# The split activations of the gate and up products: two long runs instead of sixteen interleaved pairs

## The chip, the cores and the metric

The kernel runs on one core of a Trainium2 chip. The metric is the time of one execution in device microseconds (us); lower is better. Five engines work side by side: TensorE does the matrix products (the profile calls its products PE and its weight loads PEld), VectorE is DVE, ScalarE is ACT, GpSimd is POOL, and SyncE (SP) issues most of the transfers. Operands lie in on-chip memory with 128 partitions; an address here always means a byte offset inside a partition.

## The reference, cut to what matters

One decoder block is computed for 256 tokens with 16 meta tokens ahead of them: a projection, two token mixers, a merge, and a feed-forward part. The change touches the feed-forward part alone:

```python
merged = g_a * (y_a @ w_a) + g_b * (y_b @ w_b)
h = h + merged @ w_o
gate, up = jnp.split(_rms(h, n2) @ w_gu, 2, axis=-1)      # w_gu: 2048 x 11264
return h + (jax.nn.silu(gate) * up) @ w_dn                # w_dn: 5632 x 2048
```

All inputs are float32, and the first 16 positions are dropped from the output.

## The kernel before, in words

Every large product is made from split operands. A float32 value is written as a high part, which is the value rounded to the type `float32r`, and a low part, which is the rest. A product then needs three terms: high by high, high by low, and low by high.

**Weights.** `wload` fetches a block of 1024 weights per partition into `raw` (a 512 KB transfer that SyncE issues), ACT writes the high part into `wh` (L335) and DVE the low part into `wl` (L336). There are four buffers of each of the three tiles, so the loads run a few blocks ahead of TensorE.

**Gate and up.** `cm_jobs` holds the weights still in the array and streams the activations past them. For gate and up a block is two channel tiles of 128 rows by 512 columns. The 2048 channels are 16 channel tiles, counted by `kt`. TensorE takes the four column groups `m` of a block in turn, and inside a group the two channel tiles `k`, one even and one odd. For each of these, `mm2` issues two products. The first (L441) loads a 128x128 piece of `wh` and streams 512 elements past it, 256 of the high and 256 of the low part of the activations, so that high and low results land side by side in one accumulation bank. The second (L443) loads the matching piece of `wl` and streams the 256 high elements again. For the last channel tile, 15, the order is turned round: the `wl` product first (L440), the `wh` product after it (L441). Gate and up are 11 pairs of jobs (`gt0`, `up0`, `gt1`, ...) of 8 blocks each. That is 22 x 4 x 16 = 1408 pairs of a 512-element and a 256-element product. `halves` adds up the two halves of a bank afterwards.

**The activations.** `hts` holds both parts of all 16 channel tiles. It is written once, behind the product with `w_o` (jobs `wo0` to `wo3`): each tile is transposed, scaled and split into `hts` by `post` in the `w_o` loop (ACT writes the high part, DVE the low part; both are recorded at the lines of the helper `split`, L510 and L511). Its shape is `[P, KT, 2, L]` with L = 272, although only the last 256 of the 272 elements of each row are used:

```python
hts = hp.tile([P, KT, 2, L], F32R, tag="hts", name="hts")
split(hts[:, k, 0, NMETA:], hts[:, k, 1, NMETA:], tmp)
a = act[:, kt, :, n0:n0 + n]          # in cm_jobs, with n0 = NMETA = 16, n = 256
```

So channel tiles are 2 x 272 x 4 = 2176 bytes apart, and the low part lies 1088 bytes behind the high part. In the built program the tile begins at byte 75,648 of each partition, which is 128 modulo 256. The high part of tile `kt` therefore begins at 192 modulo 256 where `kt` is even and at 64 where it is odd. The low part begins 64 further on, at 0 and at 128.

**The weights' places.** The default layout `PLACE = (0, 16, 24)` puts the pieces of `wh` at 192 and those of `wl` at 224 modulo 256, for even and odd tiles alike.

**Down.** After gate and up, the buffer of `hts` is used again as `sst` for sums of the feed-forward activations. In `w_o` and down products (`tm_jobs`, `product`) the roles are exchanged: the weights stream and the activations are held still.

The order of TensorE's instructions is the order in which the program issues them. Streams of small work are put between the products by a clock that the program keeps while it is built; nothing in it looks at addresses.

Of the kernel before, what the change touches and what calls it, by code (L numbers as in the profile page):

```python
# [10 lines left out]
F32R = mybir.dt.float32r  # L11
# [7 lines left out]
P = 128  # L19
D = 2048  # L20
NMETA = 16

T = 256
L = NMETA + T
# [3 lines left out]
DFF = 5632  # L28
# [6 lines left out]
KT = D // P  # L35
# [23 lines left out]
PLACE = (0, 16, 24)  # L59
APART = (1, 32, 32)  # L60
PLACE_T = (8, 16)

LANES = 108
BETWEEN = 2
# [52 lines left out]
def hybrid_block(ctx, tc, A, out, dbg=None):  # L117
# [18 lines left out]
    def aux_ps(name):  # L136
        return psa.tile([P, 512], F32, tag="aux", name=name)
# [88 lines left out]
    def vc(name, i=0):  # L226
        c = COLS[name] + i
        return vcol[:, c:c + 1]
# [132 lines left out]
    def kblock(ap):  # L361
        return ap.rearrange("(k p) c -> p k c", p=P)

    def mm3(ps, wh, wl, ah, al, first, last):
        nc.tensor.matmul(ps, wh, ah, start=first, stop=False)  # L365
        nc.tensor.matmul(ps, wh, al, start=False, stop=False)  # L366
        nc.tensor.matmul(ps, wl, ah, start=False, stop=last)  # L367
# [29 lines left out]
    def slot(ns):  # L397


        clock[0] += ns  # L400
        if clock[0] < clock[1]:
            return
        due = sorted((st for st in streams if st[0] <= clock[0]), key=lambda st: st[0])
        group = []
        for st in due:
            if st[2] and st[2][0] == "fox":
                mate = [c for c in streams if c[2] and c[2][0] == "chain" and st[2][1] + c[2][1] <= 8 - PSM]
                if mate and mate[0][0] > clock[0] and clock[0] < st[0] + HOLD and mate[0][0] < st[0] + HOLD:
                    continue
                group = [c for c in mate if c[0] <= clock[0]] + [st]  # L410
            else:
                group = [st]
                if st[2]:
                    group += [c for c in due if c[2] and c[2][0] == "fox" and st[2][1] + c[2][1] <= 8 - PSM][:1]
            break
        if group:
            clock[2] = 0.0
            for st in group:
                stage(st)
            clock[1] = clock[0] + max(GAP, MIX * clock[2])  # L420

    def finish_job():
        if pending:
            pending.pop()()

    def run(jobs):
        for load, mul in jobs:
            w = load()
            finish_job()
            pending.append(lambda w=w, mul=mul: mul(w))  # L430
# [6 lines left out]
    def mm2(ps, wh, wl, act, first, last):  # L437

        if last:
            nc.tensor.matmul(ps[:, :T], wl, act[:, 0, :], start=False, stop=False)  # L440
        nc.tensor.matmul(ps.rearrange("p (a t) -> p a t", a=2), wh, act, start=first, stop=last)  # L441
        if not last:
            nc.tensor.matmul(ps[:, :T], wl, act[:, 0, :], start=False, stop=False)  # L443

    def halves(dst, ps):

        nc.scalar.activation(dst, ps[:, :T], AF.Copy)
        nc.vector.tensor_tensor(dst, dst, ps[:, T:], op=ALU.add)

    def cm_jobs(wap, nk, act, n0, n, post, alloc=main_ps, name="cm", two=True, lay=PLACE):  # L450


        box = []
        cols = wap.shape[1]
        nm, kb = cols // P, 1024 // cols

        def mk(q):
            def load():
                return wload([(P, 0, [kb, cols], [((ALL,), kblock(wap[q * kb * P:(q + 1) * kb * P, :]))])], 1024,
                             lay=lay)  # L460

            def mul(w):
                (wh, wl), = w
                if q == 0:
                    box.extend(alloc(f"{name}_{m}") for m in range(nm))
                for m in range(nm):
                    ms = slice(m * P, (m + 1) * P)
                    for k in range(kb):
                        kt = q * kb + k
                        a = act[:, kt, :, n0:n0 + n]  # L470
                        if n == T and two:
                            mm2(box[m], wh[:, k % 2, k // 2, ms], wl[:, k % 2, k // 2, ms], a, kt == 0, kt == nk - 1)
                        else:
                            mm3(box[m][:, :n], wh[:, k % 2, k // 2, ms], wl[:, k % 2, k // 2, ms], a[:, 0], a[:, 1],
                                kt == 0, kt == nk - 1)
                        slot(3 * n / 2.4)
                if q == nk // kb - 1:
                    post(box)
            return load, mul
        return [mk(q) for q in range(nk // kb)]  # L480
# [28 lines left out]
    def split(hi, lo_, src):  # L509
        nc.scalar.activation(hi, src, AF.Copy)  # L510
        nc.vector.tensor_tensor(lo_, src, hi.bitcast(F32), op=ALU.subtract)  # L511
# [169 lines left out]
    def rwkv_jobs(g):  # L681
# [14 lines left out]
        for nm, off, full in (("k", 1024, True), ("v", 2048, True), ("r", 0, False)):  # L696
            n0, n = (0, L) if full else (14, T + 2)
            jobs += cm_jobs(w_in[:, off + c0:off + c0 + 256], KT, xhl, n0, n, post(nm, off, full), name=f"{nm}{g}", lay=APART)
# [512 lines left out]
    gt = None  # L1211
# [36 lines left out]
    gt = gt_pool.__enter__()  # L1248
# [52 lines left out]
    hp = hp_pool.__enter__()  # L1301
    hh = hp.tile([P, 2, D], F32, tag="hh", name="hh")

    hts = hp.tile([P, KT, 2, L], F32R, tag="hts", name="hts")
    ss2 = hp.tile([P, 2, 4], F32, tag="ss2", name="ss2")
    rs2 = hp.tile([P, 2], F32, tag="rs2", name="rs2")
    rsb2 = hp.tile([P, T], F32, tag="rsb2", name="rsb2")

    def tm_jobs(wap, nk, ah, al, post, name, lay=PLACE_T):

# [26 lines left out]
    for j in range(4):  # L1337
        js = slice(j * 512, (j + 1) * 512)
        nc.sync.dma_start(hh[:, :, js], x[:, js].rearrange("(t p) c -> p t c", p=P))

        def post(t, ps, j=j, js=js):
            nc.vector.tensor_tensor(hh[:, t, js], ps, hh[:, t, js], op=ALU.add)
            jk = hp.tile([P, 512], F32, tag="jk", name=f"jk{j}{t}", bufs=2)
            nc.scalar.activation(jk, hh[:, t, js], AF.Square, accum_out=ss2[:, t, j:j + 1])
            if t == 0:
                return
            for k in range(4 * j, 4 * j + 4):
                pt = aux_ps(f"hT{k}")[:, :T]
                for t in range(2):
                    nc.tensor.transpose(pt[:, t * P:(t + 1) * P], hh[:, t, k * P:(k + 1) * P], ident)  # L1350
                tmp = hp.tile([P, T], F32, tag="htmp", name=f"htmp{k}", bufs=3)
                nc.vector.tensor_scalar(tmp, pt, vc("n2", k), None, op0=ALU.mult)
                split(hts[:, k, 0, NMETA:], hts[:, k, 1, NMETA:], tmp)
        run(tm_jobs(A["w_o"][0][:, js], KT, mgh, mgl, post, f"wo{j}"))
    finish_job()
    nc.vector.tensor_reduce(rs2, ss2, axis=AX.X, op=ALU.add)
# [27 lines left out]
    wgu = A["w_gate_up"][0]  # L1384
    for j in range(DFF // 512):
        gs = [hp.tile([P, T], F32, tag="ga", name=f"ga{j}{m}", bufs=8) for m in range(4)]

        def post_gate(pss, gs=gs):
            for g, ps in zip(gs, pss):
                halves(g, ps)  # L1390
                nc.vector.tensor_tensor(g, g, rsb2, op=ALU.mult)
                nc.scalar.activation(g, g, AF.Silu)

        def post_up(pss, gs=gs, j=j):
            for m, (g, ps) in enumerate(zip(gs, pss)):
                ub = hp.tile([P, T], F32, tag="ub", name=f"ub{j}{m}", bufs=2)
                halves(ub, ps)
                nc.vector.tensor_tensor(ub, ub, rsb2, op=ALU.mult)
                nc.vector.tensor_tensor(ub, ub, g, op=ALU.mult)
                split(ach[:, 4 * j + m, :], acl[:, 4 * j + m, :], ub)  # L1400
        run(cm_jobs(wgu[:, j * 512:(j + 1) * 512], KT, hts, NMETA, T, post_gate, name=f"gt{j}"))
        run(cm_jobs(wgu[:, DFF + j * 512:DFF + (j + 1) * 512], KT, hts, NMETA, T, post_up, alloc=aux_ps, name=f"up{j}"))

# [5 lines left out]
    fast = FAST  # L1411
    slow = [i for i in range(NF // 2) if i not in fast]
    acp_h, acp_l = (t.rearrange("p (i k) (t c) -> p i k t c", k=2, t=2) for t in (ach, acl))
    sst = hp.tile([P, KT, 2, L], F32R, tag="hts", name="sst").rearrange("p k a t -> p (k a t)")
    sst = sst[:, :len(fast) * 6 * P].rearrange("p (i s a c) -> p i s a c", i=len(fast), s=3, a=2)

    def sums_of_pairs():
# [47 lines left out]
    def split_tiles():  # L1465
        return [wp.tile([P, WCOLS], F32R, tag=t, name=t, bufs=WB).rearrange("p (r c) -> p r c", c=L)[:, :, s:s + T]
                for t, s in zip(("wh", "wl"), PLACE_T)]

    def slow_jobs(i, cg, cs, end):
        def mk(x_):  # L1470
            def load():
                j = 2 * cg + x_
                return wload([(P, 0, [2, 512], [((ALL,), kblock(wdn[i * 256:(i + 1) * 256, j * 512:(j + 1) * 512]))])],
                             1024, lay=(None, *PLACE_T))

# [160 lines left out]
```

## Time and profile before

| | |
|---|---|
| median of 3 timed runs | 1520.99 us (1520.26 to 1521.58) |
| span of the profiled execution | 1517.7 us, from its first to its last instruction |
| TensorE products, share of the span | 99% |
| DVE, ACT | 73%, 53% |
| TensorE clock granted | full in all 40 slices |

The profiled execution gives its span alone as its own time; the timed runs lie 2.6 to 3.9 us above it, which is what stands around the first and the last instruction. The duration of a TensorE product in the trace contains a tail during which the next product already streams: products start about 0.23 and 0.12 us apart and last about 0.39 and 0.28 us. What counts is the distance from start to start.

### The profile page before, as it was taken

How to read it: one execution, taken by the hardware profiler on the slowest of the kernel's cores; microseconds unless marked ns; L12 is line 12 of the kernel's file. 1: busy time of each engine (PE TensorE's matmuls, PEld its weight loads, DVE VectorE, ACT ScalarE, POOL GpSimd, SP SyncE). 2: the span in 40 equal slices, each digit the busy share in tenths (PEclk: the TensorE clock that was granted, in tenths of full speed). 3: DMA queues.
4: the chain of work that ended last, by engine and by line, in shares of the span. 5: the costliest groups of instructions: out<-in, count | busy, mean ns of one | idle time of the engine just before them, and what ended most of it. 6: DMA issues, size and time to landing. Idle time of an engine off the chain costs nothing.

```text
span 1517.7 us, 26174 instructions
## 1 busy us (share of the span) xinstructions
PE 1509.9 (99%) x10071; PEld 1339.5 (88%) x10071; DVE 1112.0 (73%) x2009; ACT 808.3 (53%) x1230; POOL 99.3 (7%) x182
## 2 busy tenths in 40 slices
PE   9999999999999999999999999999999999999998
PEld 9999999999989888998888888888888888887887
DVE  7888699689789857875665666566566658879776
ACT  7664565475465545644554555454455545554543
POOL 2112202202202000000000000000000000000000
PEclk9999999999999999999999999999999999999999
DMA  8557456646645757777566666666666666566664
GB/s 271 166 166 212 119 156 185 170 122 173 188 127 149 223 152 214 234 231 240 181 179 192 189 187 193 191 186 192 190 187 191 193 186 182 178 211 201 213 206 138
DMA packets 210365, 283.32 MB, mean 187 GB/s; under 512 B 24320, under 2 KB 129296, under 8 KB 210240
## 3 DMA queue, kind: packets, MB, share of 16 engines
q1 hardware_dynamic: 205344, 277.25, 61.9%
q10 hardware_dynamic: 4896, 4.40, 0.9%
q8 instruction: 79, 1.29, 0.3%
q14 instruction: 46, 0.38, 0.1%
HBM read 274.36 MB, written 7.24 MB: 186 GB/s over the span
## 4 chain that ended last, share of the span: by engine, by line
PE 95%; DVE 3%; DMA 1%; issue 1%; ACT 0%; SPq 0%; DVEq 0%; ACTq 0%
PE up L441 11%; PE gt L441 11%; PE zg L441 8%; PE gt L443 5%; PE up L443 5%; PE dn L1461 4%; PE dn L1460 4%; PE dn L1462 4%; PE zg L443 4%; PE f L441 2%; PE br L365 2%; PE br L366 2%; PE br L367 2%; PE f L365 2%; PE wo L1329 2%; PE wo L1331 2%
## 5 line engine op out<-in xcount | busy, mean ns | idle before, releaser
L336 DVE TENSOR_TENSOR wl<-raw,wh 128x1024 fp32r<-128x1024 f32 x460 | 561.9, 1226 | 281.3 <-ACT wh L335 280.6
L335 ACT ACTIVATE wh<-raw 128x1024 fp32r<-128x1024 f32 x460 | 486.5, 1059 | 470.2 <-PE up L441 118.9
L441 PE MATMUL gt<-hts,wh 128*128 128x512 f32 x704 | 242.9, 393 | 0.0
L441 PE MATMUL up<-hts,wh 128*128 128x512 f32 x704 | 242.7, 392 | 0.0
L443 PE MATMUL gt<-hts,wl 128*128 128x256 f32 x660 | 184.8, 280 | 0.0
L443 PE MATMUL up<-hts,wl 128*128 128x256 f32 x660 | 184.6, 280 | 0.0
L441 PE MATMUL zg<-xhl,wh 128*128 128x512 f32 x512 | 181.2, 399 | 0.0
L441 PEld LDWEIGHTS up<-hts,wh 128*128 128x128 f32 x704 | 130.0, 188 | 25.2
L441 PEld LDWEIGHTS gt<-hts,wh 128*128 128x128 f32 x704 | 129.9, 188 | 25.1
L443 PE MATMUL zg<-xhl,wl 128*128 128x256 f32 x480 | 134.3, 280 | 0.0
L443 PEld LDWEIGHTS up<-hts,wl 128*128 128x128 f32 x660 | 125.3, 190 | 1.8
L443 PEld LDWEIGHTS gt<-hts,wl 128*128 128x128 f32 x660 | 125.3, 190 | 1.8
L441 PEld LDWEIGHTS zg<-xhl,wh 128*128 128x128 f32 x512 | 94.3, 188 | 18.7 <-issue 0.7
L1460 PE MATMUL dn<-wh,ach 128*128 128x512 f32 x282 | 110.7, 393 | 0.0
L1461 PE MATMUL dn<-wh,acl 128*128 128x512 f32 x282 | 110.6, 392 | 0.0
L1462 PE MATMUL dn<-wl,ach 128*128 128x512 f32 x282 | 110.5, 393 | 0.0
L443 PEld LDWEIGHTS zg<-xhl,wl 128*128 128x128 f32 x480 | 90.9, 189 | 1.2
L365 PE MATMUL f<-xhl,wh 128*128 128x272 f32 x256 | 75.9, 296 | 0.0
L367 PE MATMUL f<-xhl,wl 128*128 128x272 f32 x256 | 73.6, 288 | 0.0
L366 PE MATMUL f<-xhl,wh 128*128 128x272 f32 x256 | 73.6, 288 | 0.0
L1462 PEld LDWEIGHTS dn<-wl,ach 128*128 128x128 f32 x282 | 52.9, 187 | 12.3 <-DVE wl L336 0.3
L1461 PEld LDWEIGHTS dn<-wh,acl 128*128 128x128 f32 x282 | 52.9, 188 | 12.0
(493 smaller groups left out, 3056.7 us busy)
## 6 DMA issues: line engine op xcount, KB each, us to landing
raw<-in_w_gate_up_dram SPq DMA_DIRECT2D x176, 512.0 KB, 4.3
raw<-in_w_in_dram SPq DMA_DIRECT2D x160, 512.0 KB, 3.9
raw<-in_w_down_dram SPq DMA_DIRECT2D x74, 512.0 KB, 5.0
raw<-in_w_o_dram SPq DMA_DIRECT2D x32, 512.0 KB, 4.3
raw<-in_w_branch_a_dram SPq DMA_DIRECT2D x16, 512.0 KB, 4.6
raw<-in_w_branch_b_dram SPq DMA_DIRECT2D x16, 512.0 KB, 5.0
raw<-in_w_down_dram SPq DMA_DIRECT2D x28, 256.0 KB, 4.6
zgd<-zg ACTq DMA_DIRECT2D x30, 128.0 KB, 3.8
```

What stands on the lines that cost most here:

```text
L335: nc.scalar.activation(th, rr, AF.Copy)
L336: nc.vector.tensor_tensor(tl, rr, th.bitcast(F32), op=ALU.subtract)
L365: nc.tensor.matmul(ps, wh, ah, start=first, stop=False)
L366: nc.tensor.matmul(ps, wh, al, start=False, stop=False)
L367: nc.tensor.matmul(ps, wl, ah, start=False, stop=last)
L441: nc.tensor.matmul(ps.rearrange("p (a t) -> p a t", a=2), wh, act, start=first, stop=last)
L443: nc.tensor.matmul(ps[:, :T], wl, act[:, 0, :], start=False, stop=False)
L1329: nc.tensor.matmul(o, ah[:, kt, ts_], hi, start=first, stop=False)
L1331: nc.tensor.matmul(o, ah[:, kt, ts_], lo_, start=False, stop=last)
L1460: nc.tensor.matmul(o, a[0], hi, start=first, stop=False)
L1461: nc.tensor.matmul(o, a[1], hi, start=False, stop=False)
L1462: nc.tensor.matmul(o, a[0], lo_, start=False, stop=last)
```

## The change: what it does

`hts` becomes one long row per partition with two runs. The first holds the high parts of all 16 channel tiles back to back, 1024 bytes each; the second holds the low parts in the same way. Both runs are preceded by 64 unused bytes, and the whole by 128 more:

```diff
+HPART = KT * T + NMETA
+HSTART = NMETA + 32
+HTS = 2 * HPART + 32
...
-    hts = hp.tile([P, KT, 2, L], F32R, tag="hts", name="hts")
+    hts = hp.tile([P, HTS], F32R, tag="hts", name="hts")[:, HSTART - NMETA:].rearrange("p (a e) -> p a e", a=2)
+    hts = hts[:, :, NMETA:].rearrange("p a (k t) -> p k a t", t=T)
...
-                split(hts[:, k, 0, NMETA:], hts[:, k, 1, NMETA:], tmp)
+                split(hts[:, k, 0], hts[:, k, 1], tmp)
...
-        run(cm_jobs(wgu[:, j * 512:(j + 1) * 512], KT, hts, NMETA, T, post_gate, name=f"gt{j}"))
-        run(cm_jobs(wgu[:, DFF + j * 512:DFF + (j + 1) * 512], KT, hts, NMETA, T, post_up, alloc=aux_ps, name=f"up{j}"))
+        run(cm_jobs(wgu[:, j * 512:(j + 1) * 512], KT, hts, 0, T, post_gate, name=f"gt{j}"))
+        run(cm_jobs(wgu[:, DFF + j * 512:DFF + (j + 1) * 512], KT, hts, 0, T, post_up, alloc=aux_ps, name=f"up{j}"))
...
-    sst = hp.tile([P, KT, 2, L], F32R, tag="hts", name="sst").rearrange("p k a t -> p (k a t)")
+    sst = hp.tile([P, HTS], F32R, tag="hts", name="sst")
```

The tile still begins at byte 75,648. High part `kt` now begins 192 + 1024 `kt` bytes into it, which is 64 modulo 256 for every `kt`, and the low part 16,448 bytes behind the high part, at 128 modulo 256. Against before, the even channel tiles move from 192 and 0 to 64 and 128; the odd ones keep their places modulo 256. The tile shrinks from 34,816 to 33,024 bytes, so the smaller tiles allocated behind it move down by 1,792 bytes, seven times 256. `sst` begins where it began. On every engine the instructions are the same, in the same order and with the same waits; only line numbers and addresses differ.

## The prediction

> **What bounds the kernel now.** I read the page first, its busy shares, its chain and its groups; then the stretch in which gate and up run; then the time line and single instructions of TensorE in that stretch.
>
> ```profile
> span 1517.7 us, 26174 instructions
> ...
> PE 1509.9 (99%) x10071; PEld 1339.5 (88%) x10071; DVE 1112.0 (73%) x2009; ACT 808.3 (53%) x1230; POOL 99.3 (7%) x182
> ...
> PE up L441 11%; PE gt L441 11%; PE zg L441 8%; PE gt L443 5%; PE up L443 5%; PE dn L1461 4%; PE dn L1460 4%; PE dn L1462 4%; PE zg L443 4%; PE f L441 2%; PE br L365 2%; PE br L366 2%; PE br L367 2%; PE f L365 2%; PE wo L1329 2%; PE wo L1331 2%
> ...
> L441 PE MATMUL gt<-hts,wh 128*128 128x512 f32 x704 | 242.9, 393 | 0.0
> L441 PE MATMUL up<-hts,wh 128*128 128x512 f32 x704 | 242.7, 392 | 0.0
> L443 PE MATMUL gt<-hts,wl 128*128 128x256 f32 x660 | 184.8, 280 | 0.0
> L443 PE MATMUL up<-hts,wl 128*128 128x256 f32 x660 | 184.6, 280 | 0.0
> ```
>
> TensorE is busy for 99% of the span, and the chain that ended last lies on it. Four entries of the chain, 11 + 11 + 5 + 5 = 32% of the span, are the products that read `hts`. Idle time before them is 0.0. The next view gives the busy time of each engine in the stretch in which gate and up run:
>
> ```profile
> core 0: us, PE busy (x) PEld busy (x) DVE busy (x) ACT busy (x) POOL busy (x), PEclk, DMA share, GB/s
> 800.00:1289.70 489.70, 489.70 (x2810) 431.25 (x2809) 308.26 (x462) 247.48 (x359) 0.00 (x0) 1.00 0.66 189
> ```
>
> TensorE has no gap in these 489.7 us and the full clock, while DVE, ACT and the transfers have a third or more of the time to spare. The stretch is therefore as long as 1408 pairs of products take back to back. The change adds or removes no instruction; what it can alter is how far apart two products start. So I looked at that distance, in one job of gate or up:
>
> ```profile
> 900.93 0.39 PE L441 MATMUL up<-hts,wh 128*128 128x512 f32 x1
> ...
> 901.28 0.40 PE L441 MATMUL up<-hts,wh 128*128 128x512 f32 x1
> ...
> 901.63 0.39 PE L441 MATMUL up<-hts,wh 128*128 128x512 f32 x1
> ...
> 923.13 0.39 PE L441 MATMUL gt<-hts,wh 128*128 128x512 f32 x1
> ```
>
> The job that begins at 900.93 is followed by the next at 923.13. Its 64 pairs take 22.20 us, 346.9 ns each. The first row is channel tile 0, the second tile 1, the third the next even one: 0.39 and 0.40 alternate. Single instructions from the same job, in the view by tile (shortest, median and longest duration in ns; one instruction each), give this more finely:
>
> ```profile
> L441 PE MATMUL up<-hts,wh x1: 397/397/397, 903.4 to 903.4; 128*128 128x512 f32 x1
> L443 PEld LDWEIGHTS up<-hts,wl x1: 192/192/192, 903.4 to 903.4; 128*128 128x128 f32 x1
> L443 PE MATMUL up<-hts,wl x1: 278/278/278, 903.6 to 903.6; 128*128 128x256 f32 x1
> ...
> L441 PE MATMUL up<-hts,wh x1: 388/388/388, 903.7 to 903.7; 128*128 128x512 f32 x1
> L443 PEld LDWEIGHTS up<-hts,wl x1: 188/188/188, 903.7 to 903.7; 128*128 128x128 f32 x1
> L443 PE MATMUL up<-hts,wl x1: 281/281/281, 903.9 to 903.9; 128*128 128x256 f32 x1
> ```
>
> The product at 903.4 is the eighth of its job, counted in steps of 346.9 ns from 900.93, so an odd tile; the one at 903.7 is even. An odd pair lasts 397 + 278 = 675 ns and an even one 388 + 281 = 669, on average 672. Durations contain an overlap with the next product: (672 - 346.9) / 2 = 163 ns for each of the two, about the same for all, so I take differences of durations as differences of distance. This is the row that the case turns on. Two neighbours of one kind and shape differ by 9 ns, and the weight load that runs beside the longer one is longer too (192 against 188). By the addresses, an even tile streams from 192 and 0 modulo 256 and an odd one from 64 and 128, past weight pieces that lie at 192 and 224 in both cases. So the place of the streamed operand has a price here, and the change puts all tiles in the odd tiles' place.
>
> **The change part by part.** Instructions, waits, transfers and their queues stay as they are, so no term comes from them. The 16 writes of the high and 16 of the low parts keep their shape:
>
> ```profile
> L510 ACT ACTIVATE hts<-htmp x16: 417/418/423, 722.3 to 793.7; 128x256 fp32r<-128x256 f32 x16
> L511 DVE TENSOR_TENSOR hts<-htmp,hts x16: 414/418/420, 723.0 to 794.9; 128x256 fp32r<-128x256 f32 x16
> ```
>
> Sixteen durations lie within 6 ns over even and odd tiles alike, so their place has no price on these engines: zero, hidden by the `w_o` products; uncovered, 32 x 6 ns would be 0.2 us. The tiles behind `hts` move by seven times 256 bytes and keep their remainder: zero, since ACT and DVE, which use them, have slack in the stretch; `sst` does not move: zero.
>
> What is left is one term: 1408 pairs, times the time of an odd pair among odd pairs, less 672. Before the change an odd pair always stands between even ones, with one exception. At channel tile 15 the `wl` product comes first, so there an odd 512-element product follows an odd 256-element one:
>
> ```profile
> L441 PE MATMUL up<-hts,wh x1: 393/393/393, 922.9 to 922.9; 128*128 128x512 f32 x1
> L441 PE MATMUL gt<-hts,wh x1: 393/393/393, 923.1 to 923.1; 128*128 128x512 f32 x1
> ...
> L440 PE MATMUL up<-hts,wl x44: 280/282/283, 831.9 to 1278.0; 128*128 128x256 f32 x44
> ```
>
> The product at 922.9 is tile 15 behind its own `wl` product: 393, not 397. The one at 923.1 is tile 0 behind tile 15: 393 as well, not 388. So the price is not a property of the tile's own address alone; what ran just before counts as much. For the 512-element product the nearest row is 393 (same place, same predecessor; only the weight piece loaded beside it lies elsewhere). For the 256-element product there are two near rows, each with one neighbour right: 278 (behind an odd `wh` product, but with an even one next) and 282 (an odd one next, but behind an even product). I take their middle, 280. The sum: 393 + 280 = 673 against 672, so +1 ns x 1408 = +1.4 us; with 278 it is 671 and -1.4 us, with 282 it is 675 and +4.2 us. Bounds for the pair from all rows of this stretch are 388 + 278 = 666 (-8.4 us) and 397 + 282 = 679 (+9.9 us).
>
> That 512-element products average 393 whatever stands where is supported by those of the `w_o` stage, which stream weights from other places and have a wide scatter with the same middle:
>
> ```profile
> L1329 PE MATMUL wo<-wh,mgh x128: 387/394/404, 697.5 to 788.1; 128*128 128x512 f32 x128
> L1331 PE MATMUL wo<-wl,mgh x128: 390/392/479, 698.0 to 788.6; 128*128 128x512 f32 x128
> ```
>
> The sum stands against the profiled span of 1517.7 us, which lies 3.3 us below the median of 1521.0; I carry that distance over unchanged. So the span becomes 1519.1 us, and the timed median 1522.4 us. A measurement of this kernel can tell about 0.2%, 3.0 us or 2.2 ns per pair, from no change; the forecast lies inside that.
>
> One rule speaks against any effect at all. The Trainium skill, "TensorE: Matmul & The Clock Gate", section "Step-by-step: what each phase is for", says that TensorE reads the streamed operand and the weights through two independent ports, so that loading the next weights takes nothing from the running product. By that rule addresses could not matter and the time would stay at 1521.0 us. The trace does not agree as it stands: in the rows above, load and product are both longer (192 and 397 against 188 and 388) where only the place of the streamed operand differs.
>
> **The rivals.**
>
> *Slower: the odd place carries its own price.* A collision between the stream from 64 and 128 and the weight load from 224 would explain that the 397 and the 192 always come together. Then every pair lasts 397 + 278 = 675: 704 even pairs become 6 ns longer, +4.2 us, 1525.2 us. With 282 for the second product it is 679, +9.9 us, 1530.9 us. For it: the pairing of the two rows, and that no odd 512-element product of the quoted ones is under 393. Against it: the 393 at tile 15, the same place without the price. It decides the sign from 2.2 ns per pair upward.
>
> *Faster: the alternation is what costs.* The even `wl` product streams from 192 while the next `wh` piece, at 192 too, is loaded. If that delays its stream, the delay shows in the product behind it, which happens to be the odd one. After the change no product streams from where its neighbour's weights lie, and a pair lasts 388 + 278 = 666: -8.4 us, 1512.6 us; with half of this gained, 1516.8 us. For it: 281 against 278 for the 256-element products, and 397 falling to 393 when an odd product precedes. Against it: that 393 is not 388, and the even product behind an odd one, at 923.1, has 393 as well.
>
> *Nothing: places only shift time between neighbours.* Then a pair stays at 672 and the time at 1521.0 us. For it: 388 and 397 lie evenly about 393. Against it: the pair sums 669 and 675 differ, though they need not once all are alike. The rule of two ports gives the same time.
>
> **How the numbers follow.** My forecast, an odd pair at 671 to 674 ns, has 0.26, and the third rival 0.12: together 0.38 for within 0.2%. The slower rival has 0.35, of which 0.05 for the end near 679. The faster one has 0.27, about half of it at the full gain and half at the half gain. The likeliest band is the middle one, and its time from the nearest rows is 1522.4 us; alone it would reach from 1518.0 to 1524.0. The range is 1514.0 to 1527.0 us: it takes in the slower rival at 675 and the faster one up to 5 ns per pair, and leaves out the far ends of both (some 0.10 below, 0.05 above).
>
> **What would show each step.** In the profile of the changed kernel the durations of the gate and up products should no longer alternate: each of the 512- and 256-element kinds becomes one value. If the forecast is right, the 512-element group has a mean near 393, the 256-element one near 280, and the stretch of gate and up is 488 to 493 us. Means of 397 with loads of 192 on `wl` everywhere would show the slower rival, 388 and 278 with loads of 188 the faster one. Anything that differs outside that stretch, idle time of TensorE in it, or other durations of the writes to `hts`, would show that a step costed at nothing was not. The prediction would be wrong above all if a uniform stream settles in a pattern that none of the alternating rows shows.

## The result: 8.4 us slower, all of it in gate and up

| | before | after |
|---|---|---|
| median, timed in turn on one chip | 1520.78 us (1520.19 to 1521.58) | 1529.14 us (1527.92 to 1529.86) |
| span of the profiled execution | 1517.7 us | 1527.4 us |

The ratio is 1.0052, with an interval of 1.0041 to 1.0063. The forecast was 1522.4 us with a range up to 1527.0: the time lies above the range. The page of the profile after, its span, busy shares and the four groups of gate and up:

```profile
span 1527.4 us, 26174 instructions
...
PE 1518.4 (99%) x10071; PEld 1339.4 (88%) x10071; DVE 1110.9 (73%) x2009; ACT 808.1 (53%) x1230; POOL 101.3 (7%) x182
...
L445 PE MATMUL gt<-hts,wh 128*128 128x512 f32 x704 | 246.9, 395 | 0.0
L445 PE MATMUL up<-hts,wh 128*128 128x512 f32 x704 | 246.9, 395 | 0.0
L447 PE MATMUL gt<-hts,wl 128*128 128x256 f32 x660 | 185.6, 281 | 0.0
L447 PE MATMUL up<-hts,wl 128*128 128x256 f32 x660 | 185.4, 281 | 0.0
```

There are as many instructions as before and still no idle time ahead of the products, but 395 stands where 393 and 392 stood and 281 where 280 stood. To see where the time is, the span is cut at the first product of gate and at the first of down. The view by windows gives for each stretch its length, the busy time of the engines (PE, PEld, DVE, ACT, POOL), the granted clock, the share of the transfers and GB/s. Before:

```profile
0.00:788.81 788.81, 785.62 (x6232) 718.07 (x6232) 613.60 (x1295) 442.53 (x739) 99.31 (x182) 1.00 0.63 184
788.81:1278.34 489.53, 489.53 (x2828) 431.76 (x2827) 306.90 (x464) 246.85 (x356) 0.00 (x0) 1.00 0.66 189
1278.34:1517.70 239.36, 234.78 (x1015) 189.66 (x1013) 191.53 (x252) 118.90 (x136) 0.00 (x0) 1.00 0.59 189
```

After:

```profile
0.00:788.18 788.18, 784.98 (x6232) 717.08 (x6232) 612.10 (x1295) 442.18 (x739) 101.26 (x182) 1.00 0.63 184
788.18:1286.04 497.86, 497.86 (x2827) 432.95 (x2826) 307.13 (x464) 246.91 (x356) 0.00 (x0) 1.00 0.64 186
1286.04:1527.40 241.36, 235.54 (x1015) 189.42 (x1013) 191.68 (x252) 119.00 (x136) 0.00 (x0) 1.00 0.59 188
```

Gate and up take 497.9 us instead of 489.5: +8.3 us, as much as the timed medians differ (+8.4). TensorE is busy for the whole stretch and its clock is full both times. The other two stretches differ by 0.6 and 2.0 us; over all 19 profiled kernels of this study the first ran from 787.7 to 789.2 us and the last from 239.3 to 242.1, so that is scatter between executions. The spans of the two profiled executions differ by 9.7 us, more than the medians, and the one before seems to have been short: it lies 3.1 us under its median, while the five timed executions after have a span 1.7 to 1.8 us under their time. So the 3.3 us that the prediction carried over were only in part what stands around the first and the last instruction. (The prediction placed gate and up at 800 to 1290. In the profile's time they run from 788.8 to 1278.3; its sum came from the pairs of one job and does not hang on that.) On the time line after, the first products of the second and the third job:

```profile
811.71 0.40 PE L445 MATMUL up<-hts,wh 128*128 128x512 f32 x1
...
834.30 0.40 PE L445 MATMUL gt<-hts,wh 128*128 128x512 f32 x1
```

The job from 811.71 to 834.30 takes 22.59 us for its 64 pairs, 353.0 ns each, where 346.9 stood before. The 21 jobs behind the first are alike: 21 x 64 x (352.9 - 346.9) = 8.1 us. By tile, with shortest, median and longest duration, the products of `up` in the view of after:

```profile
L445 PE MATMUL up<-hts,wh x704: 387/395/396, 811.7 to 1285.8; 128*128 128x512 f32 x176
...
L447 PEld LDWEIGHTS up<-hts,wl x660: 187/188/188, 811.7 to 1285.3; 128*128 128x128 f32 x165
L447 PE MATMUL up<-hts,wl x660: 279/281/282, 811.9 to 1285.6; 128*128 128x256 f32 x165
```

The alternation is gone. A pair lasts 395 + 281 = 676 ns, and the loads of `wl` take 188, the shorter of the two values from before. But 676 is 4 ns more than 672, while the pair became 6 ns longer from start to start: durations show only part of the loss.

### The profile page after: what moved, and what is told of

Its sections match the earlier page's. It is cut to its first block, busy times and chain, and to the rows that moved or that the text cites. A ratio compares the mean times of both kernels' runs of the same rounds, so it can differ in the third digit from the quotient of the medians.

```text
span 1527.4 us, 26174 instructions
## 1 busy us (share of the span) xinstructions
PE 1518.4 (99%) x10071; PEld 1339.4 (88%) x10071; DVE 1110.9 (73%) x2009; ACT 808.1 (53%) x1230; POOL 101.3 (7%) x182
## 4 chain that ended last, share of the span: by engine, by line
PE 94%; DVE 3%; DMA 1%; issue 1%; ACT 0%; SPq 0%; DVEq 0%; ACTq 0%
PE up L445 11%; PE gt L445 11%; PE zg L445 8%; PE up L447 5%; PE gt L447 5%; PE zg L447 4%; PE dn L1466 3%; PE dn L1465 3%; PE dn L1467 3%; PE f L445 2%; PE br L369 2%; PE br L370 2%; PE br L371 2%; PE f L369 2%; PE wo L1334 2%; PE wo L1336 2%
## 5 line engine op out<-in xcount | busy, mean ns | idle before, releaser
L445 PE MATMUL gt<-hts,wh 128*128 128x512 f32 x704 | 246.9, 395 | 0.0
L445 PE MATMUL up<-hts,wh 128*128 128x512 f32 x704 | 246.9, 395 | 0.0
```

## The experiments

All of them change addresses only. A place below is a byte address modulo 256; "64/128" is a high part at 64 and a low part at 128. The step is the distance from the first product of a job to that of the next, divided by 64. Ratios are to the kernel before.

**1. All tiles at the even tiles' place, 192/0.**

```diff
-HSTART = NMETA + 32
+HSTART = NMETA
...
```

> Two long runs as in the change, but all high parts at 192 and all low parts at 0 modulo 256, the place of the even channel tiles before. Theory 'own place' (a pair costs what its own place costs): 388 + 281 = 669 ns of duration per pair, 3 less than 672, so 1516.6 us against 1520.8. Theory 'likeness' (what helped before was that the places alternate; any one place for all tiles costs about what the change measured): about 1529 us. Theory 'distance' (the 16 KB between the high and the low half of one 512-element product costs the time): about 1529 us.

Measured: 1523.46 us, ratio 1.0014 (1.0005 to 1.0023). By tile and on the time line:

```profile
L445 PE MATMUL up<-hts,wh x704: 390/394/398, 811.6 to 1279.8; 128*128 128x512 f32 x176
...
L447 PE MATMUL up<-hts,wl x660: 277/279/281, 811.8 to 1279.5; 128*128 128x256 f32 x165
```

```profile
900.79 0.39 PE L445 MATMUL up<-hts,wh 128*128 128x512 f32 x1
...
923.10 0.39 PE L445 MATMUL gt<-hts,wh 128*128 128x512 f32 x1
```

A step of 348.6 ns: neither the gain that a cheap even place would bring nor the 353 of after. Likeness of all tiles alone is not the cause of the change's 353. And 394 + 279 = 673 is 1 ns above before, the step 1.7.

**2. Two long runs, but even tiles at 192/0 and odd ones at 64/128.** The low part lies 16.7 KB behind the high part, about as after the change. `Placed` gives each channel tile `k` a place of its own in the row, with its low part `HLOW` behind it (in elements of 4 bytes).

```diff
+HLOW = 2 * 2080 + 16
...
+    hts = Placed(hp.tile([P, HTS], F32R, tag="hts", name="hts"), lambda k: 16 + k % 2 * 2080 + k // 2 * 256, HLOW)
...
```

> Long runs, the low part still 16.7 KB behind the high part, but even tiles in one pair of runs at 192 and 0, odd tiles in another at 64 and 128 modulo 256, as before the change. Theory 'place' in both its forms (own place, likeness): durations alternate again as 388/281 and 397/278, and the time is back at 1520.8 us, within 1 us. Theory 'distance': about 1529 us, no alternation needed.

Measured: 1521.28 us, ratio 0.9999 (0.9989 to 1.0009).

```profile
L457 PE MATMUL up<-hts,wh x704: 388/393/397, 811.7 to 1277.7; 128*128 128x512 f32 x176
...
L459 PE MATMUL up<-hts,wl x660: 278/280/282, 811.9 to 1277.4; 128*128 128x256 f32 x165
```

388 to 397 and 278 to 282 are the values of before, and so is the step, 346.9. The two runs cost nothing.

**3. All tiles at 64/128, the low part only 2,112 bytes behind.** The places of the change without its long distance.

```diff
+HLOW = 528
...
+    hts = Placed(hp.tile([P, HTS], F32R, tag="hts", name="hts"), lambda k: 48 + k // 2 * 1088 + k % 2 * 256, HLOW)
...
```

> All tiles at 64 and 128 modulo 256 as in the change, but the low part only 2112 bytes behind the high part and channel tiles in groups of two. Theory 'place': as the change, 1529 us within 1 us, 395 and 281 ns. Theory 'distance': about 1521 us.

Measured: 1529.63 us, ratio 1.0053 (1.0038 to 1.0068), step 352.9. On its page:

```profile
L457 PE MATMUL up<-hts,wh 128*128 128x512 f32 x704 | 246.9, 395 | 0.0
```

The same as after. With experiment 2: the remainder decides, the distance does not. The tile has its old size of 34,816 bytes here, so the small tiles behind it stand where they stood before the change: that the change moved them is not the cause either.

**4. Stream and weights both moved on by 64 bytes.**

```diff
-HSTART = NMETA + 32
+HSTART = NMETA + 48
...
+PLACE_GU = (0, 32, 40)
...
+        ... hts, 0, T, post_gate, lay=PLACE_GU, name=f"gt{j}"))
```

> As the change, but the streamed activations and the weight pieces of gate and up both 64 bytes further on (128 and 192 against 0 and 32 modulo 256): their relation is that of the change. If only the relation of stream and weights counts: 1529 us within 1 us. If the absolute place of the stream counts: a different time, which no row seen so far fixes; between 1512.6 and 1531 us.

Measured: 1529.38 us, ratio 1.0051 (1.0036 to 1.0066), step 352.9.

```profile
L446 PE MATMUL up<-hts,wh x704: 387/395/396, 811.7 to 1285.8; 128*128 128x512 f32 x176
...
L448 PE MATMUL up<-hts,wl x660: 279/281/282, 811.9 to 1285.6; 128*128 128x256 f32 x165
```

Every tile stands elsewhere, and the durations are those of after to the nanosecond. So a common shift of 64 bytes does nothing; what counts is where the stream lies relative to the weights.

**5. A map of the weights' places.** The stream stays at 64/128, and each of the 22 jobs has places of its own for `wh` and `wl`. Three kernels cover the 64 combinations, each timed once.

```diff
-... hts, 0, T, post_gate, name=f"gt{j}"))
+... hts, 0, T, post_gate, lay=(0, *PLACES[2 * j]), name=f"gt{j}"))
```

> The change's activations, all at 64 and 128 modulo 256, and other places for the weight pieces: each of the 22 jobs of gate and up has its own pair of places for wh and wl in steps of 32 bytes; this kernel has wh at 128, 160 and the first places with wh at 192 modulo 256. Each job's 64 pairs are read alone from the trace. Theory 'relation': the pair (wh 192, wl 224) gives the change's 353 ns from pair to pair; other places give other values, some under the 347 ns of before. Rival 'stream alone' (only the place of the streamed operand counts, whatever the weights' place): all 22 jobs take 353 ns per pair.

> The same with wh at 192 (the last places), 224, 0 and the first ones at 32 modulo 256. Theory 'relation': as for the first map; and if a pair's time is a sum of a term of wh's place and one of wl's place, the differences between two columns of wl are the same in every row of wh, within 1 ns. Rival 'resonance' (the two loads and the stream settle into a common rhythm): the differences change from row to row, and values repeat on a few levels.

> The same with wh at 32 (the last places), 64 and 96 modulo 256, and twice the change's own places at the end. Theory 'relation': (wh 64, wl 96) has the relation of the kernel with all tiles at 192 and 0 and gives its 348.3 ns; the two jobs at the end give 353. Rival 'stream alone': all at 353.

Measured: 1525.68, 1525.79 and 1525.39 us. Steps in ns inside the jobs, without their edges. (The first jobs of the three kernels, `wh` and `wl` at 128 and 128, 192 and 64, 32 and 0, are interrupted by small products and are read beside these.)

```
          wl 128   160    192    224      0     32     64     96
wh 128     346.7  353.3  348.9  353.3  351.1  346.7  348.9  350.0
wh 160     350.0  353.3  346.7  351.1  353.3  351.2  350.2  346.7
wh 192     350.0  353.3  350.0  348.9  351.1  349.9  348.9  346.6
wh 224     350.1  351.7  346.7  350.0  351.7  350.1  346.7  351.1
wh   0     353.3  350.0  346.7  350.0  351.1  346.7  349.9  346.7
wh  32     346.6  353.3  346.7  353.3  346.7  346.6  353.3  346.7
wh  64     348.3  350.0  346.7  349.9  348.9  346.7  353.3  348.4
wh  96     349.9  348.9  360.0  353.4  351.1  346.7  353.3  353.3
```

Three things are in it. The steps are not a scatter but lie, within 0.2 ns, on levels: 346.7 and a quarter, a third, a half, two thirds, three quarters, once and twice 6.67 ns more. The starts in the traces show what a fraction means. The steps of a job repeat after a few pairs (351, 349, 347 ns at 192 and 224; 352, 348 at 192 and 128), and one whole pattern lasts a whole number of times 6.667 ns: 346.7 is 52 of them, 353.3 is 53, and 348.9 is 157 in three pairs. Rows and columns don't add up: with `wl` at 192 the step is 346.7 in five rows and 360.0 in the last. And `wh` 64 with `wl` 96, which stands to 64/128 as the weights of experiment 1 do to 192/0, gives 348.4, close to its 348.6; inside the jobs both have the same pattern of eight steps (346, 349, 343, 349, 349, 351, 346, 353 ns).

The cell of the change itself, 192 and 224, does not fit. It ran three times, and each time at 348.9. This is one of the three, a job of the first map:

```profile
1214.92 0.39 PE L467 MATMUL up<-hts,wh 128*128 128x512 f32 x1
...
1237.27 0.40 PE L467 MATMUL gt<-hts,wh 128*128 128x512 f32 x1
```

349.2 for the whole job, at places at which the changed kernel takes 353. The changed kernel's first job has both values. This is its time line around the two small products that stand in its middle, transposes onto `prb` (eight others stand between its first products):

```profile
795.71 0.39 PE L445 MATMUL gt<-hts,wh 128*128 128x512 f32 x1
...
801.99 0.39 PE L445 MATMUL gt<-hts,wh 128*128 128x512 f32 x1
802.22 0.28 PE L447 MATMUL gt<-hts,wl 128*128 128x256 f32 x1
802.33 0.38 PE L399 MATMUL prb<-ident,ob 128*128 128x128 f32 x2
802.47 0.48 PE L445 MATMUL gt<-hts,wh 128*128 128x512 f32 x1
802.79 0.28 PE L447 MATMUL gt<-hts,wl 128*128 128x256 f32 x1
802.91 0.40 PE L445 MATMUL gt<-hts,wh 128*128 128x512 f32 x1
...
803.97 0.40 PE L445 MATMUL gt<-hts,wh 128*128 128x512 f32 x1
```

Ahead of the transposes 18 pairs take 6.28 us, 348.9 each; behind them three take 1.06 us, 353.3 each, and so it stays to the end of the stage. The same places can run in two rhythms, and here the step changes where the stream is interrupted. By tile, ahead of the transposes:

```profile
L445 PE MATMUL gt<-hts,wh x36: 392/392/394, 789.8 to 802.0; 128*128 128x512 f32 x36
L447 PE MATMUL gt<-hts,wl x35: 278/281/285, 790.0 to 801.9; 128*128 128x256 f32 x35
```

So the durations of the first rhythm add up to 392 + 281 = 673 ns, and those of the second to 676.

**6. Other weights' places in `gt1` alone.** From `up1` on everything is as in the change. If the places decide alone, these 19 jobs run at 353; if the stream keeps a rhythm once begun, they may run at 349.

```diff
-... hts, 0, T, post_gate, name=f"gt{j}"))
+... hts, 0, T, post_gate, lay=(0, 16, 16) if j == 1 else PLACE, name=f"gt{j}"))
```

> The change, but with the wl pieces of one job of 22 (gt1, the third) 32 bytes lower, at 192. In the map a job with the change's own places ran at 348.9 ns per pair three times, right behind jobs with other places; in the changed kernel the same places run at 348.9 only until the two small transposes of spread() come into job gt0, and at 353.3 from there to the end. Theory 'rhythm' (the same places allow two steady patterns, and what ran before selects one): the jobs behind gt1 run at 348.9, 19 jobs x 64 x 3.7 ns = 4.5 us less than the change, about 1524.5 us. Rival 'place alone' (each place has one cost, and something else slowed the changed kernel): the jobs behind gt1 are back at 353.3, 1529 us.

Measured: 1524.22 us, ratio 1.0027 (1.0017 to 1.0037). `gt1`, `up1` and the beginning of `gt2` on the time line:

```profile
834.51 0.40 PE L445 MATMUL gt<-hts,wh 128*128 128x512 f32 x1
...
856.91 0.39 PE L445 MATMUL up<-hts,wh 128*128 128x512 f32 x1
...
879.26 0.39 PE L445 MATMUL gt<-hts,wh 128*128 128x512 f32 x1
```

`up0` still took 352.9 per pair, `gt1` 350.0, and `up1` and all behind it 349.2, at the changed kernel's own places. Gate and up take 493.3 us instead of the 497.9 of the change: one job with another layout, 22 us long, gains 4.6 us. That the rhythm outlives its cause is thereby shown. The first job of this kernel shows something else:

```profile
791.24 0.40 PE L445 MATMUL gt<-hts,wh 128*128 128x512 f32 x1
...
801.84 0.40 PE L445 MATMUL gt<-hts,wh 128*128 128x512 f32 x1
...
802.55 0.38 PE L399 MATMUL prb<-ident,ob 128*128 128x128 f32 x2
```

30 pairs take 10.60 us, 353.3 each, ahead of the transposes. Up to there instructions and addresses are those of the change, which ran at 348.9 in this place. So the job can begin in either rhythm; what decided it is not known.

**7. The two transposes a little earlier and later.** A constant of the program's clock sets where they stand: 12000 in the change.

```diff
-SPREAD = 12000
+SPREAD = 12300
```

```diff
-SPREAD = 12000
+SPREAD = 11700
```

> The change, with the two transposes of spread() one pair of products later (behind pair 39 of job gt0 instead of 38); no other instruction moves. Theory 'rhythm': the pattern behind them can be either one; if it is the other, all of the rest runs at 348.9 and the time is about 1523.5 us, if not, 1529 us. Rival 'place alone': 1529 us, and no change of pattern at the transposes.

> The same with the transposes one pair earlier (behind pair 37). The pattern of 348.9 ns repeats after three pairs, so 37, 38 and 39 meet it at its three places. Theory 'rhythm': 1523.5 us or 1529 us, as for the later one. Rival 'place alone': 1529 us.

Measured: 1528.74 and 1529.58 us, ratios 1.0053 (1.0033 to 1.0073) and 1.0059 (1.0039 to 1.0079). The transposes start 14.5 and 13.8 us behind the first product of gate, one pair later and one earlier than in the change (14.2). Both kernels turn from 348.9 to 353.3 there and stay so, as do those of experiments 3 and 4 at their transposes. So the transposes can turn the rhythm; that they are needed is not shown, since the kernel of experiment 6 was in the slow one ahead of them and no kernel without them was run. The times don't tell the theories apart, since every position tried ended in the slow rhythm.

**8. `wl` at 96 instead of 224, in all of gate and up.** The map's place with 346.6.

```diff
+PLACE_GU = (0, 16, 56)
...
+        ... hts, 0, T, post_gate, lay=PLACE_GU, name=f"gt{j}"))
```

> The change, with the wl pieces of gate and up at 96 instead of 224 modulo 256, wh still at 192. In the map this pair of places took 346.6 ns per pair and 346.7 over a whole job, against 346.9 before the change. Theory 'relation': 1520.8 us, within 1 us, all jobs at 346.7. Rival 'stream alone' or a lasting cost of the long runs: 1529 us. If the interruption by spread() sends this place into another pattern: between 1521 and 1530 us.

Measured: 1519.92 us, ratio 0.9998 (0.9988 to 1.0008).

```profile
900.30 0.39 PE L446 MATMUL up<-hts,wh 128*128 128x512 f32 x1
...
922.49 0.39 PE L446 MATMUL gt<-hts,wh 128*128 128x512 f32 x1
```

346.7 again: one number in the weights' layout takes the whole loss back.

**9. The low part at the same remainder as the high part, 64/64, with 22 places for the weights.** 346.7 was the lowest step so far; is it a floor?

```diff
-HPART = KT * T + NMETA
-HSTART = NMETA + 32
+HPART = KT * T
+HSTART = 48
...
```

> Is 346.7 ns per pair the least that any place gives? All runs at 64 modulo 256, the low part too (16,384 bytes behind the high part instead of 16,448), and 22 pairs of places for the weights: wh at 192 and at 32 with all eight places of wl, and six more. Theory 'floor': values on the same steps as in the map (346.7, 348.9, 350.0, 351.1, 353.3), none under 346.6. Rival 'the low part's place has a price of its own': values off these steps, some at 343 to 345 or lower, and then a kernel faster than both.

Measured: 1526.59 us, once. Most jobs lay on the known levels, but one (`wh` 32, `wl` 64) ran at 344.5, a third of 6.67 below 346.7. It is no floor. Then these places for all jobs:

```diff
+PLACE_GU = (0, 40, 48)
...
```

> Uniform activations, high and low parts both at 64 modulo 256 (16,384 bytes apart), wh at 32 and wl at 64 in all jobs of gate and up: the places of the one job that took 344.5 ns per pair, 344.9 over the whole job. If that pattern holds through the transposes and from job to job: (346.9 - 344.9) x 1408 = 2.8 us less than before, 1518.0 us, ratio 0.998. If the interruption selects another pattern, or the alternation is needed for the least time: 1520.8 us or more.

Measured: 1518.15 us, ratio 0.9985 (0.9976 to 0.9994), 344.9 in every job behind the first. In the first the transposes turned it from 344.4 to 353.3, and at the border to the second job it came back. And the other 42 places in two kernels:

> High and low parts both at 64 modulo 256, 22 further pairs of places: wh at 128, 160 and 224. If places under 346.7 ns per pair are common once the low part has the remainder of the high part, two or more of these 22 are under it; if the one job was a rare case, none. All values on steps of 6.667 ns divided by a small number of pairs.

> The same with wh at 224 (last places), 0, 64 and 96. As for the other: two or more of 22 under 346.7, or none.

Measured: 1523.53 and 1523.66 us, once each. One job in each ran lower still; in the first of them, `wh` 128 and `wl` 64:

```profile
902.00 0.40 PE L467 MATMUL up<-hts,wh 128*128 128x512 f32 x1
...
923.87 0.40 PE L467 MATMUL gt<-hts,wh 128*128 128x512 f32 x1
```

341.7 for the job, 340.0 inside it: once 6.67 below 346.7. In the other it was `wh` 0 and `wl` 64, 341.4 for the job. The rest, but for the interrupted first jobs, lay from 346.7 to 353.3. Two or more low places in each kernel had been expected, or none; there was one. Some steps are new, but the rule of experiment 5 holds for them: patterns of five pairs, 348.0, 349.3, 350.7 and 352.0, are 346.7 and one to four fifths of 6.67 more.

**10. Both of these places for all jobs.**

```diff
+PLACE_GU = (0, 32, 48)
...
```

> High and low parts both at 64 modulo 256, wl at 64 as in low0, wh at 0: the places of a job that took 340.0 ns per pair and 341.4 over the whole job. If the pattern holds through the transposes and over all jobs: (346.9 - 341.4) x 1408 = 7.7 us less than before, 1512.8 us, ratio 0.995. If another pattern takes over at the transposes: 1515 to 1524 us.

```diff
+PLACE_GU = (0, 0, 48)
...
```

> The same with wh at 128: the places of the other job at 340.0 ns per pair, 341.7 over the whole job. If the pattern holds: 7.3 us less than before, 1513.2 us, ratio 0.995. If not: 1515 to 1524 us.

Measured: with `wh` at 0 1513.50 us, ratio 0.9952 (0.9939 to 0.9966), the fastest kernel of the study; with `wh` at 128 1525.89 us, ratio 1.0034 (1.0021 to 1.0046). The time line of the first, one job:

```profile
899.18 0.39 PE L446 MATMUL up<-hts,wh 128*128 128x512 f32 x1
...
921.02 0.39 PE L446 MATMUL gt<-hts,wh 128*128 128x512 f32 x1
```

341.2, and so in all later jobs, though its first job ran at 350.0 from the transposes to its end: here the border of the job turned the slow rhythm into the fast one. Of the second kernel, by tile ahead of the transposes, and then the time line of the same job as above:

```profile
L446 PE MATMUL gt<-hts,wh x19: 389/389/389, 792.7 to 798.8; 128*128 128x512 f32 x19
...
L448 PE MATMUL gt<-hts,wl x18: 276/276/276, 792.9 to 798.7; 128*128 128x256 f32 x18
```

```profile
900.47 0.40 PE L446 MATMUL up<-hts,wh 128*128 128x512 f32 x1
...
922.90 0.40 PE L446 MATMUL gt<-hts,wh 128*128 128x512 f32 x1
```

It began in the rhythm of 340.0 and kept it through its transposes, at 801.6 us; at the border to the second job it left it and ran at 350.5 to the end. The expectation for it missed by 12.7 us, and the time lies above its fallback of 1515 to 1524 us too, because the map had shown the place in one job only, and could not show which rhythm survives a border.

## Why the prediction was wrong

- *Only gate and up can change, and only by distance from start to start:* right. The writes, the moved small tiles and the stretches around came out at nothing, and TensorE had no gap.
- *The alternation disappears:* right; each kind has one value in the slow rhythm, 395 and 281.
- *One term, 393 + 280 = 673, +1 ns a pair:* this step failed. Its rows came from channel tile 15 and from between even tiles, single places inside an alternating stream; the uniform stream settled at 395 + 281 = 676 and at a step 6.0 ns longer, in a rhythm that no row of before contains. The last sentence of the prediction named that, but no chance and no time stood behind it. The forecast's sum of 673 does occur, for the 12 us ahead of the transposes (5), but with a step of 348.9, 2 ns above before, where the sum says 1.
- *The tail is the same for all, so differences of duration are differences of distance:* this failed too. The tail is (676 - 352.9) / 2 = 161.5 ns after, 162.6 before. By durations the loss would be 4 x 1408 = 5.6 us; the stage lost 8.3. Experiment 1 shows the same, 1 against 1.7 ns.
- *The slower rival, the odd place's own price, 1530.9 us at its far end:* near in time and wrong in cause. It asked for 397 and loads of 192 everywhere; the loads are 188. The same stream at the odd place ran at 360.0 and at 346.6 with other weights' places (5), and at 349.2 with the same ones (6).
- *The faster rival, that alternation costs:* refuted by the result, 676 ns and a step 6.0 ns longer where it asked for 666, and by experiment 1: there every `wl` product streams from 192, where the next `wh` piece lies, and the step of 348.6 is below the 352.9 of the change. Likeness as such neither gains nor costs: with other weights' places the same uniform stream takes 346.7 (8).
- *Nothing, and with it the rule of two independent ports in the Trainium skill, "TensorE: Matmul & The Clock Gate", "Step-by-step: what each phase is for":* by it every kernel here would take about 1521.0. With the same instructions they lie from 1513.5 to 1529.6 us. With the place of `wl` alone moved, the ratio went from the change's 1.0052 to 0.9998 (8).

What the runs show, then: the changed kernel is slower because its uniform stream, at these places relative to the weights, falls into a rhythm of 353.3 ns at the transposes in the first job and keeps it (in experiment 6 an equal beginning was in it before them); in the other rhythm of the same places it would still be slower by some 3 us, 1408 x (348.9 - 346.7). Why the unit is 6.67 ns, and what selects a rhythm, these runs don't show. That memory accesses of the stream and of the weight load get into each other's way would fit, but is only argued.

## What to carry to other kernels

Where products run back to back, compare distances from start to start over a whole repeated unit; durations hide a part. The places of the streamed high and low parts and of the weights relative to each other, modulo 256 bytes, moved this kernel by 1% from end to end, and here what they cost could not be computed from single rows: give each repeated job its own place, read many places from one profile, and then run the best ones for the whole stage, since a place can behave otherwise there. A uniform layout is not by itself the better one.

## What of the hardware was not expected

- The stream runs in a pattern of a few pairs (one to five, seven and eight were seen) that lasts a whole number of times 6.667 ns. So the mean steps lie on levels, from 340.0 to 360.0 ns: whole steps and simple fractions of 6.67 from 346.7.
- A distance of 2 KB or 16 KB between the parts makes no difference (ratio 1.0053 in experiment 3, 1.0052 in the change), and a shift of stream and weights together by 64 bytes makes none either (1.0051, experiment 4). Moving `wl` alone by 128 bytes does (0.9998, experiment 8).
- The same instructions at the same addresses have two rhythms, 348.9 and 353.3, and, in experiment 10, 340.0 and 350. Two small products or the border of a job could turn one into the other. Borders did so both ways in experiment 10, from 350 to 340.0 and from 340.0 to 350. A rhythm then lasted as long as nothing turned it, up to the end of the stage 480 us later.
